# Routing of an encoder layer: the last chunk's reciprocal root on ScalarE, and the threshold broadcast from its column

## The chip, the cores and the metric

The kernel runs on one core of one Trainium2 chip. The core has five engines with a queue of instructions each: TensorE (PE; its weight loads are shown apart as PEld), VectorE (DVE), ScalarE (ACT), GpSimd (POOL) and SyncE (SP), which here issues the transfers. The metric is the time of one launch on the device in microseconds (us); lower is better.

## The reference

One encoder layer on 512 tokens of width 1024, one batch: three token mixers in parallel, a gated sum, an output projection and a layer norm, then a mixture of 16 experts in which each expert chooses its 64 tokens. What bears on the change is the step between the norm and the experts:

```python
x = layer_norm(DN_ALPHA * x + mix, ln1_g[l], ln1_b[l])
ffn = expert_choice_ffn(x, w_router[l], w_gate_up[l], w_down[l])
...
logits = jnp.einsum('btd,de->bte', x, w_router)
aff = jax.nn.softmax(logits, axis=-1)
gate, idx = lax.top_k(jnp.swapaxes(aff, 1, 2), cap)   # cap = 64 of 512 tokens
xs = x[bidx, idx]
h = jnp.einsum('becd,edf->becf', xs, w_gate_up)
```

So the routing needs, for every token, one over the root of its variance (the norm), 16 logits and their softmax, and for every expert the 64th largest of 512 affinities as a threshold.

## The kernel before

Tokens lie in four chunks of 128 partitions (m = 0 to 3). The code is written in the order in which each engine is to issue its work; no scheduler moves anything, so each engine's queue is the order of the calls in the source.

**Output projection and router logits.** `w_rest(m, ...)` multiplies the second half of the columns of chunk m on PE (L1060 to L1062); `wo_evac` (L988, L989) adds the residual on VectorE into the place of x1 and takes norm statistics. Chunk 3 is done in two quarters, the last of 256 columns. `r_transpose` (L971, copied by ScalarE in L973) and `r_logits` (L982) give the raw logits of a chunk; the fillers `keep_warm(n)` (L1113) are n matmuls whose result nobody reads.

**Scale and softmax of a chunk.** `row_scale` aggregates the statistics on VectorE (L994), adds the epsilon (L997), and forms one over the root by an integer seed (L999, L1000) and three Newton steps of two instructions each (L1004, L1006 for one chunk). `affinity` scales the logits (L1017), takes the negated maximum (L1020), has ScalarE do the exponential with its sum (L1022), and divides (L1024, L1026). `r_back` transposes the affinities back on PE (L1031) and has ScalarE copy them (L1033) into `a01` (chunks 0, 1) or `a23` (chunks 2, 3), one row for each expert.

**Normalized tokens for the gather.** `norm_cols` (GpSimd, L1039, L1041) makes scale and bias of a chunk, `x1_norm` (ScalarE, L1044) applies them in place, and `x1_parts` splits the result: ScalarE casts the high half-precision part XH (L1047), GpSimd subtracts it to give the low part XL, in two halves of 512 columns (L1050).

**Threshold.** `rounds` finds the 64 largest of chunks 0 and 1 during the projection, and then, on `a23`, which holds them beside chunks 2 and 3, the 64 largest of all, by eight maximum instructions (L1093) with seven replacements between them (L1096). ScalarE copies one half in reverse order (`rev`, L1163), VectorE merges the halves (L1164) and takes the minimum, `cut` (L1166): one threshold for each expert in 16 partitions. ScalarE puts it on a diagonal (`dg`, L1168), and a matmul with ones (L1170) broadcasts it to 128 partitions, `thp`. VectorE compares (L1174, L1175), PE counts with a triangle of ones (L1179, L1182), VectorE makes one-hot columns (L1197).

**Gather and experts.** `gather` (L1216 with XH, L1218 with XL) picks the tokens of four experts at a time; `gate_up` (L1254) and `down` (L1287) are the expert matmuls. Their weights come through a ring of twelve places in SBUF, most of them two blocks large, in memory that earlier stages used. `ring.upto(n)` issues loads on SP (L795), each of which waits until its place is free, and `ring.done` issues a further one as soon as PE has used up a place. SP issues in order, so a load that waits holds back those behind it. The last five places are requested behind the split of the tokens (L1157): three lie in memory of the projection, the fourth in the place of x1 itself, the fifth in that of the triangle.

The order around the change is that of these lines:

```python
    keep_warm(3)
    r_transpose(3, 6, 2)
    r_back(2)
    r_logits(3, 6, 2)
    keep_warm(11)
    x1_parts(0)
    all_of(row_scale((3,), 3))
    norm_cols((3,))
    all_of(affinity((3,)))
    r_back(3)
    x1_parts(1)
    for m in (2, 3):
        x1_norm(m)
        x1_parts(m)
    keep_warm(28)
    ring.upto(len(RING))
```

Of the kernel before, what the change touches and what calls it, by code (L numbers as in the profile page):

```python
# [9 lines left out]
F32 = mybir.dt.float32  # L10
# [3 lines left out]
AF = mybir.ActivationFunctionType  # L14
ALU = mybir.AluOpType
# [3 lines left out]
P = 128  # L19
# [4 lines left out]
NEXP = 16  # L24
CAP = 64
DN_ALPHA = 2.0 ** 0.25
LN_EPS = 1e-5
# [32 lines left out]
def layer_kernel(ctx: ExitStack, tc: tile.TileContext, xt, xn, first0, wu, bgate, rpb, gains, wrt,  # L60
                 lnp, lnt, wx, csn, nmask, tri, iota, out, dbg=None):
    nc = tc.nc
# [6 lines left out]
    cp = ctx.enter_context(tc.tile_pool(name="cp", bufs=1))  # L69
# [5 lines left out]
    def R(tag, shape, name, dt=F32, bufs=None):  # L75
        return rp.tile(shape, dt, name=name, tag=tag, bufs=bufs)
# [3 lines left out]
    def PB(tag, name, shape=(P, 512)):  # L80
        return ps.tile(list(shape), F32, name=name, tag=tag, bufs=PS_BUFS[tag])

    def small(shape, name, dt=F32, bufs=2):
        return sp.tile(shape, dt, name=name, tag=name, bufs=bufs)
# [145 lines left out]
    ident = cp.tile([P, P], F32, name="ident")  # L230
# [654 lines left out]
    st_all = rt[:, 5:7].rearrange("p a b -> p (a b)")[:, :96].rearrange("p (m q s) -> p m q s", m=NT, q=4)  # L885
    ones_f = rt[:, 7:9].rearrange("p a b -> p (a b)")
# [63 lines left out]
    def x1(m):  # L950
        return X1[:, m]
# [7 lines left out]
    nc.gpsimd.memset(a23, 0.0)  # L959
    top = cp.tile([48, 64], F32, name="top")  # L960

    XT, LG = {}, {}
    mvs, rs_v, rs_h, rs_y, rs_a, nmx, sme, rce = (
        small([P, NT, 2] if n == "mv" else [P, NT], "r_" + n, bufs=1) for n in ("mv", "v", "h", "y", "a", "nm", "sm", "rc"))

    def r_transpose(m, k0, n=4):
        t = R("tmp", [P, n, P], f"x1T{m}{k0}", bufs=2)
        tp = PB("T", f"x1t{m}{k0}", (P, n, P))
        for j in range(n):
            k = k0 + j  # L970
            nc.tensor.transpose(tp[:, j], x1(m)[:, k * P:(k + 1) * P], ident)  # L971
            XT[m, k] = t[:, j]
        nc.scalar.copy(t, tp)  # L973

    def r_logits(m, k0, n=4):
        if k0 in (0, 4):
            LG[m] = PB("mm", f"lg{m}{k0}")
        lg = LG[m][:, :NEXP]
        if k0 == 4:
            nc.tensor.matmul(lg, ident, lgA[:, m], start=True, stop=False)  # L980
        for k in range(k0, k0 + n):
            nc.tensor.matmul(lg, XT.pop((m, k)), wg_t[:, k], start=(k == 0), stop=(k in (3, 7)))  # L982
        if k0 == 0:
            nc.scalar.copy(lgA[:, m], lg)

    def wo_evac(m, acc, c0, n, q):
        x = x1(m)[:, c0:c0 + n]
        nc.vector.scalar_tensor_tensor(x, x, DN_ALPHA, acc[:, :n], op0=ALU.mult, op1=ALU.add)  # L988
        nc.vector.bn_stats(st_all[:, m, q], x)  # L989

    def row_scale(ms, nq):
        c = slice(ms[0], ms[-1] + 1)
        for m in ms:
            nc.vector.bn_aggr(mvs[:, m], st_all[:, m, :nq])  # L994
        yield
        v, hv, y, a = rs_v[:, c], rs_h[:, c], rs_y[:, c], rs_a[:, c]
        nc.vector.tensor_scalar(v, mvs[:, c, 1], LN_EPS, None, op0=ALU.add)  # L997
        yield
        nc.vector.tensor_scalar(y.bitcast(I32), v.bitcast(I32), -0.5, RSQRT_SEED, op0=ALU.mult, op1=ALU.add)  # L999
        nc.vector.tensor_scalar(hv, v, -0.5, None, op0=ALU.mult)  # L1000
        yield
        for i in range(3):
            if len(ms) == 1:
                nc.vector.tensor_scalar(a, y, hv, y, op0=ALU.mult, op1=ALU.mult)  # L1004
                yield
                nc.vector.tensor_scalar(y, a, 1.5, y, op0=ALU.add, op1=ALU.mult)  # L1006
            else:
                nc.vector.tensor_tensor(a, y, y, op=ALU.mult)
                nc.vector.tensor_tensor(a, a, hv, op=ALU.mult)
                yield  # L1010
                nc.vector.scalar_tensor_tensor(y, a, 1.5, y, op0=ALU.add, op1=ALU.mult)
            yield

    def affinity(ms):
        ex = {m: LG[m][:, NEXP:2 * NEXP] for m in ms}
        for m in ms:
            nc.vector.scalar_tensor_tensor(lgA[:, m], LG.pop(m)[:, :NEXP], rs_y[:, m:m + 1], rb, op0=ALU.mult,  # L1017
                                           op1=ALU.add)
        c = slice(ms[0], ms[-1] + 1)
        nc.vector.tensor_reduce(nmx[:, c], lgA[:, c], axis=AX.X, op=ALU.max, negate=True)  # L1020
        for m in ms:
            nc.scalar.activation(ex[m], lgA[:, m], AF.Exp, bias=nmx[:, m:m + 1], accum_out=sme[:, m:m + 1])  # L1022
        yield
        nc.vector.reciprocal(rce[:, c], sme[:, c])  # L1024
        for m in ms:
            nc.vector.scalar_tensor_tensor(aff[:, m], ex[m], rce[:, m:m + 1], ones_f[:, :NEXP], op0=ALU.mult, op1=ALU.mult)  # L1026
        yield

    def r_back(m):
        ap = PB("Y", f"ap{m}")  # L1030
        nc.tensor.transpose(ap[:NEXP, :P], aff[:, m], ident)  # L1031
        p = 32 * (m % 2)
        nc.scalar.copy(a01[p:p + NEXP] if m < 2 else a23[p:p + NEXP, 64:], ap[:NEXP, :P])  # L1033
# [3 lines left out]
    def norm_cols(ms):  # L1037
        c = slice(ms[0], ms[-1] + 1)
        nc.gpsimd.tensor_scalar(r13[:, c], rs_y[:, c], X_SCALE, None, op0=ALU.mult)  # L1039
        for m in ms:  # L1040
            nc.gpsimd.tensor_scalar(nb_t[:, m:m + 1], mvs[:, m, 0:1], r13[:, m:m + 1], -1.0, op0=ALU.mult, op1=ALU.mult)  # L1041
# [4 lines left out]
    def x1_parts(m):  # L1046
        nc.scalar.copy(XH[:, m], x1(m))  # L1047
        for h in range(2):
            c = slice(h * 512, h * 512 + 512)
            nc.gpsimd.tensor_tensor(XL[:, m, c], x1(m)[:, c], XH[:, m, c], op=ALU.subtract)  # L1050
# [4 lines left out]
    def wo_part(acc, m, u, kp, c, n, last):  # L1055
        h, lo = (x.rearrange("p (k c) -> p k c", k=2) for x in u)
        tok = slice(m * P, (m + 1) * P)
        for k in range(2):
            kk = 2 * kp + k
            nc.tensor.matmul(acc, mh[:, kk, tok], h[:, k, c:c + n], start=(kk == 0), stop=False)  # L1060
            nc.tensor.matmul(acc, mh[:, kk, tok], lo[:, k, c:c + n], start=False, stop=False)
            nc.tensor.matmul(acc, ml[:, kk, tok], h[:, k, c:c + n], start=False, stop=(kk == KD - 1))  # L1062
# [18 lines left out]
    def w_rest(m, c, n, q, hooks={}):  # L1081
        acc = PB("S", f"woc{m}{c}")
        for kp in range(4):
            hooks.get(kp, lambda: None)()
            wo_part(acc[:, :n], m, us[kp], kp, c, n, kp == 3)
        wo_evac(m, acc, 512 + c, n, q)
# [16 lines left out]
    def all_of(g):  # L1103
        for _ in g:
            pass

    def then(*fs):
        return lambda: [f() for f in fs]

    def keep_warm(n):  # L1110
        warm2 = PB("T", "warm2")
        for _ in range(n):
            nc.tensor.matmul(warm2[:, :P], ident, ident, start=True, stop=True)  # L1113

    w_rest(0, 0, 512, 1, {1: lambda: r_transpose(3, 0), 2: lambda: r_logits(2, 0), 3: lambda: r_logits(3, 0)})
    w_rest(1, 0, 512, 1, {1: lambda: r_transpose(0, 4), 3: lambda: r_logits(0, 4)})
    all_of(row_scale((0, 1), 2))
    norm_cols((0, 1))
    w_rest(2, 0, 512, 1, {1: lambda: r_transpose(1, 4), 2: lambda: r_logits(1, 4),
                          3: lambda: all_of(affinity((0, 1)))})  # L1120
    s2 = row_scale((2,), 2)
    seg = rounds(a01, 0, a23[:, 0:64], True)

# [15 lines left out]
        all_of(f2)  # L1139

    w_rest(3, 256, 256, 2, {1: then(lambda: r_transpose(3, 4, 2), third), 2: lambda: r_logits(3, 4, 2)})
    keep_warm(3)
    r_transpose(3, 6, 2)
    r_back(2)
    r_logits(3, 6, 2)
    keep_warm(11)
    x1_parts(0)
    all_of(row_scale((3,), 3))
    norm_cols((3,))
    all_of(affinity((3,)))  # L1150
    r_back(3)
    x1_parts(1)
    for m in (2, 3):
        x1_norm(m)
# [9 lines left out]
    nc.vector.scalar_tensor_tensor(rev, rev, 1.0, top[:NEXP], op0=ALU.mult, op1=ALU.max)  # L1164
    cut = small([NEXP, 1], "cut", bufs=1)
    nc.vector.tensor_reduce(cut, rev, axis=AX.X, op=ALU.min)  # L1166
    dg = cp.tile([NEXP, NEXP], F32, name="dg")
    nc.scalar.activation(dg, ident[:NEXP, :NEXP], AF.Copy, scale=cut)  # L1168
    thp = PB("S", "thp")
    nc.tensor.matmul(thp[:, :NEXP], ones_f[:NEXP], dg, start=True, stop=True)  # L1170
    keep_warm(1)
    msk = cp.tile([P, NT, 2, NEXP], F16, name="msk")
    thb = thp[:, None, :NEXP].to_broadcast([P, NT, NEXP])
# [352 lines left out]
    for e in range(NEXP):  # L1526
# [50 lines left out]
        act_h(e)  # L1577
        if e % 4 == 3 and e < NEXP - 1:
            all_of(gather(e // 4 + 1))
    eps = small([P, 1], "eps", bufs=1)  # L1580
    nc.vector.memset(eps, LN_EPS)
    ch = small([P, NT, 13], "ch", F32R, bufs=1)
    nc.vector.memset(ch[:, :, 1:11:9].bitcast(F32), 1.0)
    nc.vector.memset(ch[:, :, 7:9].bitcast(F32), 0.0)
    warm_s = small([P, 1], "warm_s", bufs=1)
    nc.scalar.activation(warm_s, eps, AF.Sqrt)
    down(NEXP - 2, lambda: h_transpose(NEXP - 1, spare.rearrange("p (c n) -> p c n", c=4)))
    last_down(g2, {0: x0, 1: x1q}, spare)
# [140 lines left out]
```

## Time and profile before

| | |
|---|---|
| median of three runs | 979.08 us |
| the runs | 977.21, 979.08, 1060.49 us |
| the profiled execution, its own time | 977.92 us |
| its span | 976.1 us |
| instructions in the span | 13068 |
| PE busy | 944.4 us |
| DVE busy | 451.9 us |
| ACT busy | 274.3 us |
| POOL busy | 78.4 us |
| bytes moved by the DMA engines | 251.62 MB |

The span is what the profiler recorded of one execution; its own time has 1.8 us more around it. The profile page gives busy time by engine, the span in 40 slices, the chain of work that ended last, and groups of instructions by line. In a timeline each line is a stretch of instructions of one engine: start, length, engine, line, operation, the tile written and the tiles read, shapes and number, and in brackets how long the engine was idle before it and on what that wait ended. Instructions of one engine overlap a little at their ends, so the next one can start before the length given is over. Times within the span are counted from its start.

### The profile page before, as it was taken

How to read it: one execution, taken by the hardware profiler on the slowest of the kernel's cores; microseconds unless marked ns; L12 is line 12 of the kernel's file. 1: busy time of each engine (PE TensorE's matmuls, PEld its weight loads, DVE VectorE, ACT ScalarE, POOL GpSimd, SP SyncE). 2: the span in 40 equal slices, each digit the busy share in tenths (PEclk: the TensorE clock that was granted, in tenths of full speed). 3: DMA queues.
4: the chain of work that ended last, by engine and by line, in shares of the span. 5: the costliest groups of instructions: out<-in, count | busy, mean ns of one | idle time of the engine just before them, and what ended most of it. 6: DMA issues, size and time to landing. Idle time of an engine off the chain costs nothing.

```text
span 976.1 us, 13068 instructions
## 1 busy us (share of the span) xinstructions
PE 944.4 (97%) x5350; PEld 615.0 (63%) x5350; DVE 451.9 (46%) x857; ACT 274.3 (28%) x540; POOL 78.4 (8%) x86
## 2 busy tenths in 40 slices
PE   8999899999999999999999999999999998997996
PEld 8899787889888888887886333433343332432344
DVE  6347678765376566237464155331332222231426
ACT  5343345444354454323223000100010000100123
POOL 0002403000032231000013000000000000000003
PEclk9999999999999999999999999999999999999998
DMA  9312121111333322584719999999999999999992
GB/s 357 111 68 65 65 65 44 65 44 58 85 117 111 101 82 75 217 325 183 279 50 389 389 422 430 430 433 429 429 430 430 430 430 431 432 429 431 428 419 100
DMA packets 38473, 251.62 MB, mean 258 GB/s; under 512 B 12543, under 2 KB 12927, under 8 KB 24590
## 3 DMA queue, kind: packets, MB, share of 16 engines
q1 hardware_dynamic: 37982, 249.74, 63.5%
q10 hardware_dynamic: 432, 1.05, 0.3%
q8 instruction: 42, 0.69, 0.3%
q14 instruction: 17, 0.14, 0.0%
HBM read 247.89 MB, written 2.10 MB: 256 GB/s over the span
## 4 chain that ended last, share of the span: by engine, by line
PE 70%; DMA 18%; DVE 6%; ACT 2%; POOL 2%; issue 1%; SPq 0%; DVEq 0%; POOLq 0%; ACTq 0%
DMA w<-in_wx 17%; PE g L1254 7%; PE u L1254 7%; PE y L1287 6%; PE gate L269 4%; PE gate L271 4%; PE gate L270 4%; PE nqk L271 1%; PE nqk L270 1%; PE nqk L269 1%; PE gy L627 1%; PE pr L269 1%; PE pr L270 1%; PE pr L271 1%; PE ga L1216 1%
## 5 line engine op out<-in xcount | busy, mean ns | idle before, releaser
L1254 PE MATMUL g<-w,xs 128*64 128x512 f32 x512 | 134.7, 604 | 7.5 <-DMA w<-in_wx 7.5
L1254 PE MATMUL u<-w,xs 128*64 128x512 f32 x512 | 131.6, 592 | 0.0
L1287 PE MATMUL y<-w,hT 128*64 128x512 f32 x480 | 107.0, 594 | 4.6 <-DMA w<-in_wx 3.9
L87 ACT CAST y<-y 64x512 fp32r<-64x512 f32 x30 | 17.4, 579 | 240.3 <-PE y L1287 229.0
L88 DVE TENSOR_TENSOR y<-y,y 64x512 fp32r<-64x512 f32 x30 | 20.7, 689 | 135.2 <-ACT y L87 135.2
L1254 PEld LDWEIGHTS u<-w,xs 128*64 128x64 f32 x512 | 36.8, 137 | 73.1 <-issue 71.7
L1287 PEld LDWEIGHTS y<-w,hT 128*64 128x64 f32 x480 | 33.7, 137 | 74.4 <-issue 63.4
L88 DVE TENSOR_TENSOR los<-raw_twin,whi 128x1024 fp32r<-128x1024 f32 x43 | 54.0, 1257 | 51.3 <-ACT whi L87 51.0
L271 PE MATMUL gate<-xh,los 128*128 128x512 f32 x192 | 74.8, 390 | 0.0
L1254 PEld LDWEIGHTS g<-w,xs 128*64 128x64 f32 x512 | 31.3, 136 | 63.7 <-issue 48.0
L269 PE MATMUL gate<-xh,whi 128*128 128x512 f32 x160 | 63.6, 398 | 0.0
L270 PE MATMUL gate<-xl,whi 128*128 128x512 f32 x160 | 62.4, 390 | 0.0
L1357 DVE TENSOR_TENSOR acc<-acc,cb 128x512 f32<-128x512 f32 x56 | 35.4, 683 | 34.5 <-PE cb L1355 34.5
L87 ACT CAST whi<-raw_twin 128x1024 fp32r<-128x1024 f32 x43 | 45.2, 1051 | 7.3 <-PE wo L1062 4.4
L88 DVE TENSOR_TENSOR los<-raw_twin,los 128x1024 fp32r<-128x1024 f32 x21 | 27.4, 1305 | 36.6 <-ACT los L87 36.5
L1426 POOL TENSOR_TENSOR acc<-acc,ln2g 128x512 f32<-128x512 f32 x6 | 7.6, 1279 | 435.4 <-issue 433.4
L271 PEld LDWEIGHTS gate<-xh,los 128*128 128x128 f32 x192 | 36.1, 188 | 7.7
L603 ACT ACTIVATE att_twin<-gs,nm 128x512 f32<-128x512 f32 x32 | 21.7, 683 | 51.4 <-DVE nm L602 51.4
L1264 ACT ACTIVATE tg<-g 128x512 f32<-128x512 f32 x16 | 9.6, 597 | 94.0 <-PE g L1254 94.0
L1275 DVE COPY hT<-ht 128x512 f32<-128x512 f32 x15 | 10.4, 690 | 54.6 <-PE ht L1272 54.6
L269 PEld LDWEIGHTS gate<-xh,whi 128*128 128x128 f32 x160 | 30.0, 188 | 7.5 <-issue 1.0
L270 PEld LDWEIGHTS gate<-xl,whi 128*128 128x128 f32 x160 | 30.1, 188 | 5.9
(405 smaller groups left out, 1883.9 us busy)
## 6 DMA issues: line engine op xcount, KB each, us to landing
w<-in_wx SPq DMA_DIRECT2D x86, 2048.0 KB
raw_twin<-in_wu SPq DMA_DIRECT2D x65, 512.0 KB
w<-in_wx SPq DMA_DIRECT2D x20, 1024.0 KB
raw<-in_wu SPq DMA_DIRECT2D x8, 512.0 KB
xr<-in_xt SPq DMA_DIRECT2D x4, 512.0 KB
macc<-in_xn SPq DMA_DIRECT2D x2, 1024.0 KB
first<-in_first SPq DMA_DIRECT2D x4, 384.0 KB
bf<-in_rpb SPq DMA_DIRECT2D x64, 24.0 KB
```

The costliest lines, as they stand in the source:

```text
L87: nc.scalar.copy(hi, src)
L88: nc.vector.tensor_tensor(lo, src, hi.bitcast(F32), op=ALU.subtract)
L269: nc.tensor.matmul(acc, w_h, rh[:, k], start=(k == 0), stop=False)
L270: nc.tensor.matmul(acc, w_h, rl[:, k], start=False, stop=False)
L271: nc.tensor.matmul(acc, w_l, rh[:, k], start=False, stop=(k == nk - 1))
L603: nc.scalar.activation(self.p[:, h], self.s[h], AF.Exp, bias=nm[:, h:h + 1], accum_out=self.sm[:, h:h + 1])
L627: nc.tensor.matmul(self.y[h * 64:h * 64 + 64, :P], ST["vg"][:, kc, kvh * 64:kvh * 64 + 64], self.pt[:, h, kc], start=(kc == 0), stop=(kc = ...
L1216: nc.tensor.matmul(g, XH[:, m, c], oh[:, m], start=(m == 0), stop=False)
L1254: nc.tensor.matmul(GU[e][b][hf * 64:hf * 64 + 64], xs, w[b][:, hf * 512:hf * 512 + 512], start=(k == 0), stop=(k == KD - 1))
L1275: nc.vector.tensor_copy(t, tp)
L1287: nc.tensor.matmul(y[o * 64:o * 64 + 64], hT[:, c, hf * 64:hf * 64 + 64], w[j][:, o * 512:(o + 1) * 512], start=(k == 0 and j == 0), stop= ...
L1357: nc.vector.tensor_tensor(a, a, cb, op=ALU.add)
```

## The change

Only the root of the last chunk (m = 3) and the broadcast of the threshold are done in another way; chunks 0 to 2 keep `row_scale`. The new `last_scale` has ScalarE take the root of variance plus epsilon, VectorE its reciprocal, and one Newton step follows with the half-variance formed beside it. The root belongs to another set of activation tables than the exponential, so the program has a table load ahead of a dummy root behind `w_rest(3, 256, ...)`, and another ahead of a dummy exponential behind the real root. Both dummies are activations of one column into `warm_s`, from `eps`; these two tiles are made earlier for that, `eps` on GpSimd.

In the order of the calls, `r_back(2)` goes behind the logits and the root of chunk 3, the fillers there go from 11 to 9, and the split of chunk 0 (one cast on ScalarE and two subtractions on GpSimd) goes from ahead of the root to behind `r_back(3)`.

For the broadcast, `dg` is gone: PE takes `cut`, repeated along 128 columns, as the weights and the 16 by 16 identity as the moving operand.

```diff
+    eps = small([P, 1], "eps", bufs=1)
+    nc.gpsimd.memset(eps, LN_EPS)
+    warm_s = small([P, 1], "warm_s", bufs=1)
...
+    def last_scale(m, nq):
+        c = slice(m, m + 1)
+        y, a, hv = rs_y[:, c], rs_a[:, c], rs_h[:, c]
+        nc.vector.bn_aggr(mvs[:, m], st_all[:, m, :nq])
+        nc.scalar.activation(rs_v[:, c], mvs[:, m, 1:2], AF.Sqrt, bias=eps)
+        nc.scalar.activation(warm_s, eps, AF.Exp)
+        nc.vector.tensor_scalar(hv, mvs[:, m, 1:2], LN_EPS, -0.5, op0=ALU.add, op1=ALU.mult)
+        nc.vector.reciprocal(y, rs_v[:, c])
+        nc.vector.tensor_scalar(a, y, hv, y, op0=ALU.mult, op1=ALU.mult)
+        nc.vector.tensor_scalar(y, a, 1.5, y, op0=ALU.add, op1=ALU.mult)
...
     w_rest(3, 256, 256, 2, {1: then(lambda: r_transpose(3, 4, 2), third), 2: lambda: r_logits(3, 4, 2)})
+    nc.scalar.activation(warm_s, eps, AF.Sqrt)
     keep_warm(3)
     r_transpose(3, 6, 2)
+    r_logits(3, 6, 2)
+    last_scale(3, 3)
     r_back(2)
-    r_logits(3, 6, 2)
-    keep_warm(11)
-    x1_parts(0)
-    all_of(row_scale((3,), 3))
+    keep_warm(9)
     norm_cols((3,))
     all_of(affinity((3,)))
     r_back(3)
+    x1_parts(0)
     x1_parts(1)
...
-    dg = cp.tile([NEXP, NEXP], F32, name="dg")
-    nc.scalar.activation(dg, ident[:NEXP, :NEXP], AF.Copy, scale=cut)
     thp = PB("S", "thp")
-    nc.tensor.matmul(thp[:, :NEXP], ones_f[:NEXP], dg, start=True, stop=True)
+    nc.tensor.matmul(thp[:, :NEXP], cut.to_broadcast([NEXP, P]), ident[:NEXP, :NEXP], start=True, stop=True)
...
-    eps = small([P, 1], "eps", bufs=1)
-    nc.vector.memset(eps, LN_EPS)
...
-    warm_s = small([P, 1], "warm_s", bufs=1)
     nc.scalar.activation(warm_s, eps, AF.Sqrt)
```

## The prediction

> **What bounds the kernel now.** I read the page first, then the chain of waits, then the busy time in stretches around the routing, then the timelines of the five queues there.
>
> ```profile
> span 976.1 us, 13068 instructions
> ...
> PE 70%; DMA 18%; DVE 6%; ACT 2%; POOL 2%; issue 1%; SPq 0%; DVEq 0%; POOLq 0%; ACTq 0%
> ```
>
> ```profile
> 778.67 36.36 DMA w<-in_wx
> ...
> 924.76 21.97 DMA w<-in_wx
> ```
>
> ```profile
> 509.00:524.00 15.00, 13.39 (x131) 12.45 (x130) 10.59 (x46) 8.24 (x14) 9.49 (x10) 0.95 1.01 413
> ...
> 531.50:536.00 4.50, 4.50 (x28) 1.89 (x24) 0.54 (x1) 0.00 (x0) 0.00 (x0) 1.00 0.68 226
> 536.00:556.00 20.00, 20.00 (x108) 7.33 (x108) 4.60 (x15) 2.23 (x5) 0.00 (x0) 1.00 0.98 380
> ...
> 578.00:700.00 122.00, 121.40 (x590) 47.25 (x590) 41.46 (x68) 12.20 (x21) 0.00 (x0) 1.00 1.01 430
> ```
>
> The stretches give busy time of PE, PEld, DVE, ACT and POOL, then granted clock, DMA share and GB/s. From about 556 us the expert weights come at 430 GB/s with the DMA engines full, and the chain ends in those transfers (778 to 947 us). So the end is set by bytes, counted from the last moment at which the transfers ran dry. That moment lies just behind the routing:
>
> ```profile
> w<-in_wx SPq DMA_DIRECT2D x86, 2048.0 KB
> ```
>
> ```profile
> 508.05 1.28 SPq L795 DMA_DIRECT2D w<-in_wx  x3
> 521.63 0.33 SPq L795 DMA_DIRECT2D w<-in_wx  x1
> 532.40 0.33 SPq L795 DMA_DIRECT2D w<-in_wx  x1
> 543.78 0.33 SPq L795 DMA_DIRECT2D w<-in_wx  x1
> ```
>
> The loads from 532.40 on wait until PE has used up ring blocks 0, 1, 2, so they are issued by the gather and the first expert. In 531.5 to 536 us only 226 GB/s flow, in 536 to 556 us 380. PE is busy without a break there. Hence what the routing gains or loses before the first gather matmul (L1216) passes one for one to those issues, and so to the end.
>
> The routing itself, on VectorE, ScalarE, TensorE and GpSimd:
>
> ```profile
> 509.21 0.24 DVE L994 BATCH_NORM_AGGREGATE r_mv<-rt 128x2 f32<-128x18 f32 x1
> ...
> 509.92 0.27 DVE L1004 TENSOR_SCALAR r_a<-r_y,r_h 128x1 f32<-128x1 f32 x1
> 510.23 0.21 DVE L1006 TENSOR_SCALAR r_y<-r_a,r_y 128x1 f32<-128x1 f32 x1
> ...
> 511.66 0.23 DVE L1017 SCALAR_TENSOR_TENSOR rt<-lg,r_y,rt 128x16 f32<-128x16 f32 x1
> 511.93 0.17 DVE L1020 TENSOR_REDUCE r_nm<-rt 128x1 f32<-128x16 f32 x1
> 512.56 0.16 DVE L1024 RECIPROCAL r_rc<-r_sm 128x1 f32<-128x1 f32 x1 [0.47 <-ACT lg L1022]
> 512.76 0.23 DVE L1026 SCALAR_TENSOR_TENSOR rt<-lg,r_rc,rt 128x16 f32<-128x16 f32 x1
> ...
> 519.11 0.35 DVE L1093 MAX8 top<-a 48x8 f32<-48x192 f32 x1
> ...
> 519.99 0.21 DVE L1166 TENSOR_REDUCE cut<-rev 16x1 f32<-16x64 f32 x1
> ```
>
> ```profile
> 506.91 0.19 ACT L1022 ACTIVATION_READ_ACCUMULATOR lg<-rt,r_nm 128x1 f32 x1
> 509.30 0.37 ACT L973 COPY x1T<-x1t 128x256 f32<-128x256 f32 x1 [2.20 <-PE x1t L971]
> 509.56 0.25 ACT L1033 COPY a<-ap 16x128 f32<-16x128 f32 x1
> 509.72 1.04 ACT L1047 CAST xhl<-macc 128x1024 f16<-128x1024 f32 x1
> 512.13 0.28 ACT L1022 ACTIVATE lg<-rt,r_nm 128x16 f32<-128x16 f32 x1 [1.37 <-DVE r_nm L1020]
> ...
> 513.73 1.05 ACT L1047 CAST xhl<-macc 128x1024 f16<-128x1024 f32 x1
> 514.68 1.24 ACT L1044 ACTIVATE macc<-macc,lnnb,lnr 128x1024 f32<-128x1024 f32 x1
> 515.95 1.05 ACT L1047 CAST xhl<-macc 128x1024 f16<-128x1024 f32 x1
> ...
> 518.17 1.05 ACT L1047 CAST xhl<-macc 128x1024 f16<-128x1024 f32 x1
> 519.50 0.20 ACT L1163 COPY rev<-top 16x64 f32<-16x64 f32 x1 [0.28 <-DVE top L1093]
> 520.24 0.31 ACT L1168 ACTIVATE dg<-ident,cut 16x16 f32<-16x16 f32 x1 [0.53 <-DVE cut L1166]
> ```
>
> ```profile
> 513.25 6.41 PE L1113 MATMUL warm<-ident 128*128 128x128 f32 x56
> 520.59 0.39 PE L1170 MATMUL thp<-dg,rt 16*128 16x16 f32 x2 [0.93 <-ACT dg L1168]
> ...
> 524.67 1.06 PE L1218 MATMUL ga<-oh,xhl 128*128 128x256 f16 x4
> ```
>
> ```profile
> 514.86 6.74 POOL L1050 TENSOR_TENSOR xhl<-macc,xhl 128x512 f16<-128x512 f32 x6 [1.09 <-ACT xhl L1047]
> ```
>
> VectorE is one dependent chain from 509.21 to the threshold, with ScalarE in it four times (exp 512.13, the copy of r_back(3) ahead of the sort, rev 519.50, dg 520.24). What the 2% of ScalarE in the chain hides: from 513.7 on it is full here. Its last cast ends at 518.17 + 1.05 = 519.22, only 0.28 us ahead of rev.
>
> **The change, part by part.** Times are on the clock of the profiled execution.
>
> *The root.* Before, from bn_aggr (509.21) to the scaled logits (511.66): 2.45 us. After: bn_aggr 0.24 ends at 509.45; the ScalarE root can start when the x1T copy lets it, at 509.56 as the copy behind it did before; a 128x1 activation takes 0.20 (row below), so 509.76. Then reciprocal to next 0.20 (512.56 to 512.76), first Newton half to second 0.31 (509.92 to 510.23), second half to the logits about 0.32 as now (L1006 before L1017, taken as 0.3): with one 0.03 hop the logits stand at 510.61. The half-variance product runs beside the root. Gain here 1.05 us. The maximum then ends near 511.05, and exp would start at 511.08 if ScalarE were free.
>
> *The two table loads.* Root and exponential stand in different table sets, so ScalarE loads one ahead of the root and the other behind it. The one load inside the kernel:
>
> ```profile
> 937.76 1.28 ACT L1586 ACT_TABLE_LOAD   x1
> 939.38 0.20 ACT L1586 ACTIVATE warm_s<-eps 128x1 f32<-128x1 f32 x1 [0.34 <-DVE ch L1584]
> ```
>
> A load is 1.28 us, and the 0.34 behind it is put down to VectorE's memsets, so its own cost lies between 1.28 and 1.62. The first load starts after the third chunk's exp (507.10) and ends with its dummy root at 508.58 to 508.92, inside the 2.20 us in which ScalarE waits for the transposes: free, with 0.4 us to spare. The second starts at 509.77, ends at 511.05 to 511.39, then the dummy exp (about 0.15 until the next can enter) and the copy of r_back(2) (0.16, from 509.56 to 509.72): exp starts at 511.4, at the latest 511.7. So of 1.05 us 0.74 is left (0.4 at the upper end). I take 1.28, since the trace names another cause for the idle time.
> The Trainium skill's page ScalarE: Activation LUTs (What ACT_TABLE_LOAD costs) speaks against this: a switch is 1283 ns of load plus about 1380 ns of draining, 2.66 us. Load row and page agree on 1.28; the drain isn't in the trace, where the load starts 0.02 us after the tanh and the next activation 0.34 after it. By the page, exp would start 1.3 us later than before, and the estimate would be 979.5 us instead of the sum below.
>
> *Cast and subtractions of chunk 0 moved.* The cast at 509.72, formerly in a gap, now follows r_back(3). With exp 0.74 earlier r_back(3)'s copy, the sort and the first cast start 0.74 earlier: first cast 512.99. Steps: cast to next 0.95 (513.73 to 514.68), norm to cast 1.27 (514.68 to 515.95). Two casts, norm, cast, norm: the fourth cast starts at 512.99 + 0.95 + 0.95 + 1.27 + 0.95 + 1.27 = 518.38 and ends at 519.43. The sort is done at 519.46 - 0.74 = 518.72, but rev stands behind the cast: 519.38 (a copy enters some 0.1 us before the end of its forerunner), against 519.50. So 0.6 us of the gain is lost to the moved cast; what is late next is ScalarE. With the later exp, rev is at 519.72.
>
> *GpSimd.* Its norms of chunk 3 come earlier, at no cost. All eight subtractions now follow the first cast: 514.04 + 8 x 1.123 (6.74 / 6) = 523.0, against 521.6. Two things wait for that. The matmuls with the low part (L1218) begin at 524.67: 1.6 us of cover, less the 0.5 that they come earlier. And the load at 521.63 waits for GpSimd's last reading of x1's place, with the next load queued behind it on SP; they move to 523.0. The three loads of 508.05 (2048 KB each, 6.29 MB) from 509 us at 413 GB/s last until 524.2, so the DMA engines miss at most a microsecond, and the dry spell behind (226 GB/s) absorbs it, since the next load is issued only at about 532: nothing.
>
> *PE.* r_back(2) goes behind the logits, which wait for the x1T copy anyway; four fewer filler matmuls shorten the fillers to the earlier r_back(3): nothing. Cover gone, each would delay r_back(3) by a matmul or two.
>
> *The threshold.* dg goes; before, cut ends at 520.20 and the broadcast starts at 520.59, 0.39 us. After, PE starts 0.04 behind cut: 0.35 saved. The operands change places, but both weight loads waited for dg already; I take the same matmul time.
>
> *At the end of the kernel* a memset leaves VectorE, and the dummy root no longer waits the 0.34 us; ScalarE is off the chain there, which stands in the transfers until 947 us: nothing. With the cover gone it would be a gain of 0.34.
>
> *Sum:* 519.50 - 519.38 = 0.12, plus 0.35: the broadcast starts at 520.12, 0.47 us earlier (0.13 with the later exp). The profiled execution took 977.92 with 976.1 of span; it becomes 977.45. The median shown, 979.08, lies 1.2 above it and its neighbour at 977.21; by the middle of the two undisturbed ones, 978.15, it would be 977.7. I predict 977.6.
>
> **The rivals.** *A load holds ScalarE longer than its row (slower).* For: it is one row, and the 0.34 could be its own. Against: the trace names the memset. If each load cost twice 1.28, the first ends with its dummy at 509.86, the root comes at 510.12, the second ends at 512.88, exp starts at 513.2: 1.07 late; first cast 514.80, fourth ends 521.24, rev 521.2, broadcast 521.9: 1.3 us late, 979.2. It decides from 0.47 us more per second load.
> *TensorE's clock.*
>
> ```profile
> 522.50:523.00 0.50, 0.50 (x5) 0.50 (x5) 0.43 (x3) 0.00 (x0) 0.00 (x0) 0.52 0.92 393
> ...
> 525.50:526.00 0.50, 0.50 (x5) 0.35 (x3) 0.22 (x1) 0.00 (x0) 0.00 (x0) 0.57 1.05 426
> ```
>
> The granted clock is half for 3.1 us behind the idle time around the broadcast. Fillers now end at 519.66 - 0.74 = 518.92, the broadcast comes at 520.12: 1.20 us idle instead of 0.93. That can lengthen the fall; another 3.1 us at half cost 1.6, net 979.0. A shifted phase could also spare it: 975.9.
> *ScalarE doesn't bind* (casts fit ahead of rev): 1.05 + 0.35 = 1.4, so 976.5. Against it stand the cast rows of 1.05 and the norm of 1.24.
> *Nothing arrives:* the end depends on the loads at 508 us alone, 977.9. Against it stand the 226 GB/s after 531.5.
>
> **How the numbers follow.** Forecast 0.45 (own range 977.1 to 978.0 for the profiled execution); longer loads 0.17; longer fall of the clock 0.12, spared fall 0.08; ScalarE free 0.08; nothing arrives 0.10. The range goes from the lower run less a spared fall, 977.2 - 1.6 = 975.6, to the upper run plus the longer loads, 979.1 + 1.3 = 980.4. All cases lie far inside 2% (19.6 us, about what a measurement of this kernel can tell from no change): within 0.95; 0.02 faster and 0.03 slower for what I don't see.
>
> **What would show it.** Root at 509.5 and 0.20; second table load 1.28 with exp at 511.4; rev released by its own engine, not by the sort; the fourth cast ending near 519.4; last subtraction and the load behind it near 523; first low-part matmul not waiting for GpSimd. Wrong: idle time behind a load, a longer stretch at half clock, or the load at 532.40 not moving with the broadcast.

## The result and the profile after

The changed kernel takes 982.53 us (median of seven runs, 981.04 to 985.61) against 978.34 us for the kernel before (seven runs). The ratio is 1.0040 with a 95% interval of 1.0026 to 1.0053: 4.2 us slower, only 0.4%, but with an interval that leaves no change out. A gain of half a microsecond was forecast, and the time lies above the range. (The run of 1060.49 us in the table above is over 8% longer than the other six and is in no ratio; why it was so long isn't known.) The profiled execution took 982.89 us, with a span of 981.1.

The routing did much of what was forecast. First VectorE, then ScalarE, PE and GpSimd of the changed kernel. The stretch ahead of the change took 0.71 us longer in this execution, so times are compared from the start of bn_aggr: 509.92 here, 509.21 before.

```profile
509.92 0.23 DVE L1020 BATCH_NORM_AGGREGATE r_mv<-rt 128x2 f32<-128x18 f32 x1
...
510.61 0.16 DVE L1024 RECIPROCAL r_y<-r_v 128x1 f32<-128x1 f32 x1 [0.27 <-ACT r_v L1021]
...
511.44 0.23 DVE L1031 SCALAR_TENSOR_TENSOR rt<-lg,r_y,rt 128x16 f32<-128x16 f32 x1
...
520.68 0.21 DVE L1181 TENSOR_REDUCE cut<-rev 16x1 f32<-16x64 f32 x1
...
523.10 0.80 DVE L1198 TENSOR_TENSOR rt<-rt 128x64 f32<-128x64 f32 x1
523.94 1.43 DVE L1210 TENSOR_TENSOR oh<-iota_t,rt 128x256 f16<-128x256 f32 x4
```

```profile
510.28 0.30 ACT L1021 ACTIVATE r_v<-r_mv,eps 128x1 f32<-128x1 f32 x1
510.60 1.28 ACT L1022 ACT_TABLE_LOAD   x1
511.89 0.20 ACT L1022 ACTIVATE warm_s<-eps 128x1 f32<-128x1 f32 x1
512.00 0.24 ACT L1047 COPY a<-ap 16x128 f32<-16x128 f32 x1
512.14 0.26 ACT L1036 ACTIVATE lg<-rt,r_nm 128x16 f32<-128x16 f32 x1
...
519.12 1.04 ACT L1061 CAST xhl<-macc 128x1024 f16<-128x1024 f32 x1
520.19 0.20 ACT L1178 COPY rev<-top 16x64 f32<-16x64 f32 x1
```

```profile
520.95 0.39 PE L1183 MATMUL thp<-ident,cut 16*128 16x16 f32 x2 [1.28 <-DVE cut L1181]
...
524.44 1.35 PE L1229 MATMUL ga<-oh,xhl 128*128 128x256 f16 x4
```

```profile
514.86 8.96 POOL L1064 TENSOR_TENSOR xhl<-macc,xhl 128x512 f16<-128x512 f32 x8 [2.88 <-ACT xhl L1061]
```

The broadcast comes 11.03 us behind bn_aggr instead of 11.38, so 0.35 us earlier. Its lead is nearly gone at the first gather matmul: 14.52 against 14.61, from this row of before:

```profile
523.82 1.06 PE L1216 MATMUL ga<-oh,xhl 128*128 128x256 f16 x4
```

The addition that makes pos (L1198) takes 0.80 us and ends at 523.90, 0.08 us behind GpSimd's last subtraction (514.86 + 8.96 = 523.82); the same one took 0.22 before:

```profile
522.74 0.22 DVE L1185 TENSOR_TENSOR rt<-rt 128x64 f32<-128x64 f32 x1
```

Even the 0.09 us at the gather are owed to TensorE's clock. It was granted at half around the gather of both traces, and before it held the gather back by 0.35 us (shown in the last section). In a trace of the old order without that fall the gather starts 14.26 us behind bn_aggr, so the changed routing, at 14.52, is rather 0.26 us slower (from the first one-hot to the gather it is 0.50 us here and 0.48 there, so the clock hardly holds it here): 0.35 gained at the broadcast, some 0.6 lost at the addition.

The 4 us come from behind the routing. In the stretches, as they were shown of before, the last column tells where:

```profile
531.50:536.00 4.50, 4.50 (x26) 1.74 (x23) 0.54 (x1) 0.01 (x1) 0.00 (x0) 1.00 0.92 337
536.00:556.00 20.00, 20.00 (x110) 7.49 (x109) 4.59 (x15) 2.23 (x5) 0.00 (x0) 1.00 0.97 381
578.00:700.00 122.00, 121.25 (x592) 47.20 (x590) 41.87 (x69) 11.85 (x21) 0.00 (x0) 1.00 1.01 428
```

The chain still ends in the transfers, now from 779 to 951 us:

```profile
779.07 39.08 DMA w<-in_wx
...
929.18 22.25 DMA w<-in_wx
```

The load that opens the expert stage (532.40 before) is issued here at 532.82, 22.90 us behind bn_aggr: 0.29 us earlier than before, and 0.43 later than in the trace without the fall of the clock (22.47). So the stream of weights starts within half a microsecond of where it did, and ends 4 us later. The DMA engines are as full as before, and move less: 600 to 900 us, before (first) and changed (second), DMA share and GB/s in the last two columns:

```profile
600.00:900.00 300.00, 291.99 (x1450) 114.35 (x1448) 81.15 (x152) 30.85 (x54) 0.00 (x0) 1.00 1.01 430
```

```profile
600.00:900.00 300.00, 289.55 (x1436) 112.88 (x1434) 80.85 (x151) 30.88 (x54) 0.00 (x0) 1.00 1.01 427
```

The records of single packets show it more sharply. Nearly every weight packet brings 16 KB or 8 KB into one partition. Behind 560 us, the 16 KB packets take 611 ns in 99% of the cases before. Changed, they take 612 or 613 mostly, and 618 to 621 for a quarter: 616.6 in the mean against 612.5; the 8 KB packets take 314.0 against 309.4. That is 4.1 ns x 9115 + 4.6 ns x 2304 = 48 us of packet time on 16 DMA engines, 3.0 us each.

The slow packets aren't there from the start. Of the 16 KB packets that start between 570 and 590 us, 87% still take 612 ns or less in the changed kernel (99% before); of those between 600 and 610 us only 15% do (100% before). The DMA engines are full in both stretches. The lag grows along the rest of the stream: counted in 16 KB packets, the changed kernel is 0.9 us behind before at 588 us and 3.4 us behind at 913 us (0.7 of both come from ahead of bn_aggr).

Nothing in the code of the loads changed. What did change is where their destinations lie. `dg` was a tile of 16 by 16 words, 64 bytes in each partition, in the pool that stands ahead of the large tiles. Without it everything behind moved 64 bytes down: the lowest place of the ring from byte 8960 to byte 8896, and all others likewise. 8960 is 35 x 256, and the other places too began at multiples of 256; 8896 isn't even a multiple of 128.

### The profile page after: what moved, and what is told of

Its sections match the earlier page's. It is cut to its first block, busy times and chain, and to the rows that moved or that the text cites. A ratio compares the mean times of both kernels' runs of the same rounds, so it can differ in the third digit from the quotient of the medians.

```text
span 981.1 us, 13059 instructions
## 1 busy us (share of the span) xinstructions
PE 946.3 (96%) x5346; PEld 615.4 (63%) x5346; DVE 451.3 (46%) x851; ACT 277.7 (28%) x544; POOL 79.6 (8%) x87
## 4 chain that ended last, share of the span: by engine, by line
PE 70%; DMA 18%; DVE 6%; ACT 3%; POOL 2%; issue 1%; SPq 0%; DVEq 0%; POOLq 0%; ACTq 0%
DMA w<-in_wx 18%; PE g L1267 7%; PE u L1267 7%; PE y L1300 6%; PE gate L269 4%; PE gate L271 4%; PE gate L270 4%; PE nqk L271 1%; PE nqk L269 1%; PE nqk L270 1%; PE gy L627 1%; PE pr L269 1%; PE pr L270 1%; PE pr L271 1%; PE ga L1229 1%
```

## The experiments

Two theories. **Place**: packets into places that don't begin on a certain multiple of bytes take longer, and the lost 64 bytes are the whole loss. **Late loads**: the moved cast lets GpSimd's subtractions end later, two weight loads are issued later (at 523.85 us against 521.63), and the stream loses there. The row of the changed kernel:

```profile
523.85 0.81 SPq L795 DMA_DIRECT2D w<-in_wx  x2
```

The times given are medians, against runs of the kernel before on the same chip. The ratios, with 95% intervals, are worked out from all those runs and need not be the quotient of the two medians.

### The changed kernel with its 64 bytes back

```diff
+    cp.tile([NEXP, NEXP], F32, name="pad")
     thp = PB("S", "thp")
```

> The changed kernel with an unused tile of 64 bytes a partition kept where dg stood, so that every weight place of the ring begins at byte 8960 and so on (a multiple of 256) again instead of 64 bytes lower. Theory of the place: the 16 KB packets take 611 ns again instead of 612 to 620, and the time is that of before less the 0.3 us that the routing gained, about 978.0 us. Theory of the late loads (the subtractions on GpSimd end later, so two weight loads are issued later): no difference to the changed kernel, about 982.5 us.

Measured: 978.70 us against 978.03, ratio 1.0006 (0.9996 to 1.0016): no difference to before. An unused tile takes the loss away; the two loads are as late as in the changed kernel (13.95 us behind bn_aggr, 13.93 there, 12.42 before). The 16 KB packets take 611 ns again (99%). The expected gain of 0.3 us doesn't show either, within an interval from 0.4 us faster to 1.6 us slower; by the traces there is none at the gather.

### The kernel before with the ring 64 bytes lower

```diff
-    dg = cp.tile([NEXP, NEXP], F32, name="dg")
+    dg = small([NEXP, NEXP], "dg", bufs=1)
```

> The kernel before with dg in the pool of small tiles behind the ring, nothing else: the ring begins 64 bytes lower, at 8896, as in the changed kernel. Theory of the place: packets of 612 to 620 ns and about 982.5 to 983 us. Theory of the late loads: 978.3 us, since order and waits are those of before.

Measured: 982.0 us against 978.03, ratio 1.0038 (1.0023 to 1.0052). The order of every engine is that of before, and the whole loss is there.

```profile
600.00:900.00 300.00, 289.59 (x1436) 112.90 (x1432) 80.43 (x151) 30.89 (x54) 0.00 (x0) 1.00 1.01 427
```

With these two the theory of the late loads falls.

### The two halves of the change, with the places of before

```diff
     # root and order as changed
+    dg = cp.tile([NEXP, NEXP], F32, name="dg")
+    nc.scalar.activation(dg, ident[:NEXP, :NEXP], AF.Copy, scale=cut)
     thp = PB("S", "thp")
-    nc.tensor.matmul(thp[:, :NEXP], cut.to_broadcast([NEXP, P]), ident[:NEXP, :NEXP], start=True, stop=True)
+    nc.tensor.matmul(thp[:, :NEXP], ones_f[:NEXP], dg, start=True, stop=True)
```

> Root, Newton step and the order of the calls as changed, dg and its matmul as before; places as before. Theory of the place: the casts hold rev back, and its 0.06 us of loss leave 978.4 us, the same as before. Theory of the late loads: 982 us or more, since the subtractions end as late as in the changed kernel.

Measured: 979.16 us against 978.03, ratio 1.0006 (0.9993 to 1.0018). The root and the order alone are worth nothing that can be measured here.

```diff
     # root and order as before; the tile dg stands, unused
-    nc.scalar.activation(dg, ident[:NEXP, :NEXP], AF.Copy, scale=cut)
     thp = PB("S", "thp")
-    nc.tensor.matmul(thp[:, :NEXP], ones_f[:NEXP], dg, start=True, stop=True)
+    nc.tensor.matmul(thp[:, :NEXP], cut.to_broadcast([NEXP, P]), ident[:NEXP, :NEXP], start=True, stop=True)
```

> The broadcast from the column alone, the root and the order as before; the tile dg stands unused, so the places are those of before. Theory of the place: 0.35 us faster, about 978.0 us. Theory of the late loads: the same 978.0 us. If the matmul with the column as weights were the cost: slower than before.

Measured: 977.59 us against 978.03, ratio 0.9994 (0.9985 to 1.0003). In the interval, so not shown by the time; in its trace the broadcast starts 0.06 us behind the end of the column instead of 0.39:

```profile
519.28 0.21 DVE L1166 TENSOR_REDUCE cut<-rev 16x1 f32<-16x64 f32 x1
```

```profile
519.55 0.39 PE L1169 MATMUL thp<-ident,cut 16*128 16x16 f32 x2 [0.59 <-DVE cut L1166]
```

### Which multiple counts

Three further places, in the kernel before: 128 bytes up, 32 bytes up, 256 bytes down.

```diff
     dg = cp.tile([NEXP, NEXP], F32, name="dg")
+    cp.tile([NEXP, 32], F32, name="pad")        # in the second: [NEXP, 8]
```

> The kernel before with an unused tile of 128 bytes a partition behind dg: the ring begins at 9088, a multiple of 128 but not of 256. If the boundary that counts is 256 bytes: packets over 611 ns and about 982 us, as with 8896. If it is 128 or 64 bytes: 611 ns and 978.0 us.

Measured: 981.31 us against 978.4, ratio 1.0032 (1.0021 to 1.0043). A multiple of 128 is not enough.

> The kernel before with an unused tile of 32 bytes a partition behind dg: the ring begins at 8992, a multiple of 32 alone. If only crossing the 256-byte boundary counts: as with 8896, about 982 us. If each finer boundary missed costs more: over 983 us. If a multiple of 32 is enough: 978.0 us.

Measured: 982.27 us against 978.4, ratio 1.0039 (1.0025 to 1.0054): as with 8896. A multiple of 32 is not enough.

```diff
-    top = cp.tile([48, 64], F32, name="top")
+    top = small([48, 64], "top", bufs=1)
```

> The kernel before with the tile top (256 bytes a partition) in the pool of small tiles, nothing else: the ring begins 256 bytes lower, at 8704, again a multiple of 256. If the multiple of 256 counts: packets of 611 ns and 978.4 us, the same as before. If any other place than 8960 is slower, or if a tile's move into the other pool is what cost time with 8896: about 982 us.

Measured: 978.50 us against 978.18, ratio 1.0005 (0.9996 to 1.0013). A tile's move into the other pool costs nothing that shows, nor does another multiple of 256. Rows of 600 to 900 us for 128 up, 32 up and 256 down:

```profile
600.00:900.00 300.00, 290.47 (x1440) 113.75 (x1440) 81.72 (x152) 30.89 (x54) 0.00 (x0) 1.00 1.01 427
```

```profile
600.00:900.00 300.00, 289.41 (x1438) 113.10 (x1434) 80.77 (x151) 30.89 (x54) 0.00 (x0) 1.00 1.01 426
```

```profile
600.00:900.00 300.00, 291.70 (x1448) 114.10 (x1448) 81.09 (x151) 30.89 (x54) 0.00 (x0) 1.00 1.01 430
```

All places together, with the packets behind 560 us (weight packets, ns, mean; the share is that of the 16 KB packets that take 612 ns or less):

| lowest place | left over from 256 | 16 KB | share | 8 KB | ratio |
|---|---|---|---|---|---|
| 8960 (before) | 0 | 612.5 | 99.5% | 309.4 | 1 |
| 8704 (256 down) | 0 | 613.3 | 98.8% | 309.4 | 1.0005 |
| 8896 (changed) | 192 | 616.6 | 20.8% | 314.0 | 1.0040 |
| 8896 (before, dg moved) | 192 | 616.2 | 20.3% | 314.0 | 1.0038 |
| 9088 (128 up) | 128 | 615.8 | 41.4% | 313.8 | 1.0032 |
| 8992 (32 up) | 32 | 616.8 | 10.2% | 315.0 | 1.0039 |

So the loss comes with the offset in every run, and goes with it. But the offset alone doesn't make a packet slow. The place that is filled first (at byte 25344 before and 25280 in the changed kernel, as the program lays it out) is loaded at about 465, 556 and 604 us. In the changed kernel 89%, 91% and then 16% of its packets take 612 ns or less, before 99%, 92% and 100%. With the ring 64 bytes lower in the kernel before it is the same (93%, 97%, 16%). Only from about 570 us (32 up) or 590 us (the others) on are most packets slow; what begins there wasn't tried. Nor do the runs move the ring alone: every tile behind dg moves with it, and it is the times of the packets that tie the loss to the transfers.

### Where the routing's gain went

Two edits of the changed kernel with its 64 bytes back. The first calls the split of chunk 0 behind the dummy root, so that its cast fills ScalarE's wait for the transposes:

```diff
     nc.scalar.activation(warm_s, eps, AF.Sqrt)
+    x1_parts(0)
     keep_warm(3)
...
     r_back(3)
-    x1_parts(0)
     x1_parts(1)
```

> The changed kernel with the unused 64-byte tile in dg's place, and the split of chunk 0 called right behind the dummy root instead of behind r_back(3). By the casts and GpSimd's place: the cast delays the x1T copy and so the root by 0.27 us, but rev goes by the sort again, 0.4 us earlier against the statistics than in the changed kernel; GpSimd's last subtraction ends some 2 us earlier, so the addition that makes pos takes 0.22 us again instead of 0.8; gather 1.0 us earlier than in the changed kernel, about 977.2 us. If the casts and GpSimd don't matter: 0.27 us later than the changed kernel with the tile, 979.0 us.

Measured: 977.62 us against 978.4, ratio 0.9989 (0.9978 to 1.0001), the lowest ratio of all, though its interval just reaches 1. In its trace rev is released by the sort again, the broadcast comes 10.49 us behind bn_aggr (508.46) instead of 11.38, the addition takes 0.23 us, and the gather starts 1.24 us earlier than before (13.37 against 14.61). Of these, 0.35 are the clock, which doesn't fall here; against the 14.26 of the old order without the fall it is 0.89:

```profile
516.86 1.05 ACT L1061 CAST xhl<-macc 128x1024 f16<-128x1024 f32 x1
518.19 0.20 ACT L1178 COPY rev<-top 16x64 f32<-16x64 f32 x1 [0.28 <-DVE top L1107]
```

```profile
518.95 0.39 PE L1184 MATMUL thp<-ident,cut 16*128 16x16 f32 x2 [0.59 <-DVE cut L1181]
521.83 1.28 PE L1230 MATMUL ga<-oh,xhl 128*128 128x256 f16 x4
```

```profile
521.09 0.23 DVE L1199 TENSOR_TENSOR rt<-rt 128x64 f32<-128x64 f32 x1
```

The second leaves GpSimd where it is in the changed kernel and takes one of the addition's two operands out of SBUF:

```diff
-    nc.vector.tensor_tensor(cnt, cnp, msk, op=ALU.mult)
-    nc.vector.tensor_tensor(pos, cnt[:, :, 0], cnt[:, :, 1], op=ALU.add)
+    cnt1 = PB("Y", "cnt1")[:, :NT * NEXP].rearrange("p (m e) -> p m e", m=NT)
+    nc.vector.tensor_tensor(cnt[:, :, 0], cnp[:, :, 0], msk[:, :, 0], op=ALU.mult)
+    nc.vector.tensor_tensor(cnt1, cnp[:, :, 1], msk[:, :, 1], op=ALU.mult)
+    nc.vector.tensor_tensor(pos, cnt[:, :, 0], cnt1, op=ALU.add)
```

> The changed kernel with the unused 64-byte tile, and the product before pos in two halves, the second into PSUM, so that the addition has one input in SBUF instead of two; GpSimd still subtracts at that time. If the addition waits because two inputs in SBUF and GpSimd's reading exclude each other: 0.22 us for it instead of 0.83, the one-hot columns 0.4 us earlier against the broadcast, about 978.2 us. If it is GpSimd's running as such: still 0.8 us or, with the additional product, later than before, about 978.9 us.

Measured: 978.23 us against 978.4, ratio 1.0003 (0.9992 to 1.0014), so the time tells nothing; the trace does:

```profile
523.92 0.22 DVE L1201 TENSOR_TENSOR rt<-rt,cnt 128x64 f32<-128x64 f32 x1
524.17 1.70 DVE L1213 TENSOR_TENSOR oh<-iota_t,rt 128x256 f16<-128x256 f32 x4
```

```profile
515.61 8.97 POOL L1064 TENSOR_TENSOR xhl<-macc,xhl 128x512 f16<-128x512 f32 x8 [2.88 <-ACT xhl L1061]
```

The addition is short while GpSimd still subtracts (until 524.58). The next VectorE instruction with both operands in SBUF, the first one-hot, now waits instead: four take 1.70 us, not 1.43. Where the addition was long, it ended 0.08 us behind the last subtraction, in the changed kernel as with its 64 bytes back (522.90 and 522.82) and with root and order alone (522.66 and 522.58). So it is the two operands in SBUF beside GpSimd's work, as expected, and not GpSimd's running as such; but taking it away from one instruction hands half of it to the next.

## Why the prediction was wrong, step by step

- **What bounds the kernel**: right. The end is set by bytes counted from the last dry moment, and the first ring loads moved with the routing. That a gain of the routing passes one for one to the end is shown by no run: the largest, 0.89 us at the gather, came with a ratio whose interval reaches 1.
- **The step that failed is the last one of that argument**: "the expert weights come at 430 GB/s" was taken as given for the changed kernel, and so was "dg goes" as the end of dg's account. dg was counted as an instruction of ScalarE. It was also 64 bytes of memory ahead of the ring. Without them the rate is 427 GB/s from about 600 us on. Over the 350 us from there to the end of the transfers 3 / 430 is 2.4 us, and the packet times behind 560 us give 3.0. The sum had no term for this, no rival held it, and the range ended 2.1 us below the result.
- **Root**: 1.40 us from bn_aggr to the logits forecast, 1.52 measured; the root takes 0.30 us, not the 0.20 of the dummy activation.
- **Table loads**: right. 1.28 us, and the next activation 0.01 behind the load's end, in both places; the 0.34 of before were the memsets. The load at the end of the kernel shows the same, 942.24 + 1.28 and 943.53:

```profile
942.24 1.28 ACT L1596 ACT_TABLE_LOAD   x1
943.53 0.20 ACT L1596 ACTIVATE warm_s<-eps 128x1 f32<-128x1 f32 x1
```

  The rival of the longer loads falls with it. The trace doesn't bear out the Trainium skill's ScalarE: Activation LUTs (What ACT_TABLE_LOAD costs) on about 1380 ns of drain behind a load. The exponential starts 2.22 us behind bn_aggr instead of 2.92: 0.70 earlier, 0.74 forecast.
- **The moved cast**: right in kind. rev is held by ScalarE's last cast; 0.12 us of the 0.7 was forecast to arrive there, 0.02 did (10.27 against 10.29 behind bn_aggr). The early split shows what that place costs: 0.5 us more lead at the broadcast (10.49 against 11.03).
- **GpSimd's later end, put at "nothing"**: wrong, though by tenths. The loads behind the subtractions and the low-part matmuls were covered, as forecast. A third thing wasn't looked for: VectorE's addition, now within the longer subtractions, takes 0.58 us more. That is more than the broadcast's 0.35 us, so nothing of the forecast gain was left at the gather.
- **Broadcast**: 0.35 us forecast, 0.33 measured.
- **Dry spell absorbs the late loads**: right. 531.5 to 536 us carry 337 GB/s instead of 226 (306 in the old order without the fall of the clock), and the 64 bytes back leave nothing to explain.
- **TensorE's clock**: neither rival came. The fall of before lasts 3.4 us by the slices shown (granted clock 0.52 and 0.57 at its two ends, half between), not the 3.1 of the prediction, and in the changed kernel from 522 to 526 us it is again 0.57.

What stays open: of the 4.2 us the packets explain 3.0, which lies within the interval of the loss (2.5 to 5.2 us). Single traces can't settle the rest: bn_aggr starts between 508.5 and 510.9 us in the traces here. The four in which the granted clock is half for 3.4 us early on, at 12 or about 100 us (changed, the ring 64 lower, 128 up, and the addition with PSUM), have 509.9 to 510.9, the other seven 508.5 to 509.5. Why packets into the moved places are slow only from some 40 to 60 us after the expert stage opens, and why some then take 2 ns more and others 9, wasn't tried.

The Trainium skill's DMA: Bandwidth & Descriptors (How a descriptor splits into AXI transactions) puts the boundary at 256 bytes: a transfer is cut into transactions of 256 bytes from 256-byte addresses, and one that begins elsewhere needs one more. The runs agree on the boundary: 128 isn't enough, another 256 is. What it states doesn't tell why most loads into the same places ahead of 590 us take 611 ns. The page speaks of reading, and here the written side moved. By an estimate from that page, one transaction more on 64 makes a 16 KB packet 1.6% longer; measured are 0.7%.

The Trainium skill's SBUF — State Buffer (Who interferes with whom) states that a VectorE instruction with two SBUF inputs contends with a GpSimd instruction that reads SBUF, and that this contention is an exclusive lock. The addition's 0.80 us, and 0.22 with one operand in PSUM, agree.

## What to carry to other kernels

In a kernel whose end is a stream of transfers, an edit that adds or removes a small tile is an edit of every address behind it: look at where the stream's places begin before and after, keep them on the multiple that cost nothing (256 bytes here), and put small tiles behind the large ones, so that the next edit doesn't move them. A fixed packet time in the records (611 ns in 99% of the packets) that begins to scatter says so at once, where the share of busy time says nothing. When work moves to a full engine and ends later, look for instructions that get longer beside it (here an addition of two operands in SBUF), not only for those that wait for its result. And before two traces are compared over a stretch of a few us, look whether the granted clock is the same in it.

## What the runs showed of the hardware

Bytes of places: with places off a multiple of 256 bytes (by 32, 128 or 192) a weight packet took 3.3 to 5.6 ns more in the mean behind 560 us, of 16 KB as of 8 KB, and the kernel 0.3 to 0.4% more. Most loads into the same places ahead of about 590 us took 611 ns all the same.

The fall of TensorE's clock that was a rival isn't tied to the order of the instructions: from 522 to 526 us the granted clock (third column from the end) is 0.57 before, and 1.00 with the same order and dg moved, in which the idle time around the broadcast is the same 0.93 us. At half clock the fillers ahead of the gather take 1.80 us instead of 1.14 and hold it: it starts 3.23 us behind the broadcast before, and 2.88 there (524.19 from 521.31; bn_aggr is at 509.93). The stretch and the fillers, first before, then with dg moved:

```profile
522.00:526.00 4.00, 4.00 (x35) 3.31 (x32) 2.17 (x7) 0.00 (x0) 0.00 (x0) 0.57 1.00 420
```

```profile
522.23 1.80 PE L1113 MATMUL warm<-ident 128*128 128x128 f32 x8
```

```profile
522.00:526.00 4.00, 3.68 (x53) 2.77 (x51) 2.10 (x8) 0.00 (x0) 0.31 (x1) 1.00 1.02 428
```

```profile
522.95 1.14 PE L1113 MATMUL warm<-ident 128*128 128x128 f32 x8
524.19 1.27 PE L1216 MATMUL ga<-oh,xhl 128*128 128x256 f16 x4
```
